# Half projections placed ahead of the turns of x, one transpose in another PSUM bank, and a tie on the sixth row of W_out

## The chip, the cores and the metric

The kernel is one program on one core of a Trainium2 chip. The core has a matrix engine (PE, whose weight loads are listed apart as PEld), a vector engine (DVE), a scalar engine (ACT), a general engine (POOL), and a queue (SP) that does nothing in this kernel but start transfers between the chip's large memory and the on-chip memory SBUF. PE writes its results to PSUM, which has eight banks. Each engine works through its own list of instructions in order and waits at an instruction until the data and the buffers that it needs are there.

The metric is the time of one launch in microseconds on the device. Lower is better. Three runs of the kernel before gave 1722.09, 1722.20 and 1724.09 us, so the median is 1722.2 us.

## The reference

One decoder layer over 1024 tokens with 16 learned tokens in front, width 1024:

```python
xn = rms_norm(h, mix_pre_g[l])
proj = xn @ w_in[l]                       # z, xbc, dt, q, k, v
y_ssd = ssd_mixer(z, xbc, dt_raw, ...)    # 16 heads, chunks of 128, state 128, causal conv of 4
y_sb = rms_norm(stick_breaking_attention(q, k, v), sb_norm_g[l])   # 16 heads of 64
mix = jnp.concatenate([y_ssd, y_sb], axis=-1) @ w_out[l]
h = h + rms_norm(mix, mix_post_g[l])
xn = rms_norm(h, ffn_pre_g[l])
gu = xn @ w_up[l]
g = causal_dwconv(gu[..., :D_FF], ffn_conv_w[l], ffn_conv_b[l])
f = (jax.nn.gelu(g, approximate=True) * gu[..., D_FF:]) @ w_down[l]
h = h + rms_norm(f, ffn_post_g[l])
```

Everything is float32. In stick-breaking attention the weight of key s for query t is sigmoid(q.k/8) times the product of (1 - sigmoid) over the keys between s and t; a scan along the keys gives the product.

## The kernel before

**Products.** Large products run in a fast 32-bit mode. Each operand is split into a high part (a rounded copy, made on ACT) and a low part (the rest, made on DVE or POOL), and three products high-high, low-high and high-low are summed in one PSUM bank. So every block of weights costs a load into `wraw` (two buffers), a copy on ACT (`wh`) and a subtraction (`wl`).

**The head (lines 310 to 348).** x is loaded in nine pieces: the 16 learned tokens and eight blocks of 128. For each piece i, ACT sums the squares, POOL makes the root, DVE scales the piece into `xn` (line 276, two buffers), PE turns it in eight transposes (`turn_x`, line 288, `xtp`), ACT copies the high part and DVE subtracts the low part (lines 293 and 295) into `xs`. `xs` has three thirds of 400, 384 and 256 tokens: pieces 0 to 3, 4 to 6, and 7 and 8. Between the turns PE also projects the first third for dt, for block B0 and for block C0. `conv_chain(..., True)` gives a projection in half chains of 12 matmuls each (line 169, `pj_B` and `pj_C`); the second half of a third ends with a copy on ACT (line 215). In this stretch the order of every engine is written out by hand: what the code traces first is issued first. In the kernel before, the half chains come at the end of iterations 5 to 8, behind `turn_x` of the same iteration.

**The scan (lines 482 to 712).** Convolved B, C and x blocks are turned to token order by `to_tokens`: three parts, one transpose of 16 tokens and twice four transposes of 128, each part in a bank of the pair `tp` and copied out by DVE (lines 487 and 492, `tt_B`). The pair `z` serves the decay matrices of the scan (`sg`, line 634). Outside the hand-written stretches a planner orders the instructions when the program is built, from costs that it assumes, and an instruction can be issued ahead of others that were traced before it.

**Attention and W_out (lines 770 to 1080).** Eight head pairs p, eight query blocks i, written (p,i). A block has its score matmuls (`z`, line 782, in the pair of double banks `zz`), two sigmoids on ACT (`kp` and `bt`, lines 783 and 784), a scan on DVE (line 790), products on POOL (lines 792 and 793), then two blocks later its weights are turned on PE (`tw`, line 804, also in `zz`) and copied by ACT (`th`, line 806), and one block after that multiplied with v (`av`, line 819). PE's order is written out by hand here; that of ACT, DVE and POOL is the planner's. While the last two head pairs run, the first half of W_out is prepared: eight rows of blocks, each a load into one of the two `wraw` buffers (line 892), a scaled copy on ACT (line 904) and a subtraction on DVE (line 905). `STAGE` sets after which block each row is traced: row 5 at (6,6), row 6 at (6,7), row 7 at (7,0), row 8 at (7,1). Rows 7 and 8 take the place of the last third of `xs`, which is free once v of the last pair is projected. The row that is traced at (6,6) stands inside `tc.issue_after(copied[0])`, which keeps its ACT instruction behind the latest `th` copy that was traced; at (6,6) that is the last copy of block (6,4), at (6,7) the last copy of block (6,5).

**After that** come the two halves of W_out, the up projection with seven products per pair of blocks in place of eight, and the down projection, all bound by PE.

Of the kernel before, what the change touches and what calls it, by code (L numbers as in the profile page):

```python
# [17 lines left out]
P = 128  # L18
# [39 lines left out]
def tile_layer(ctx: ExitStack, tc: tile.TileContext, x, meta, rows, parts,  # L58
# [22 lines left out]
    def psum_z(name):  # L81
        return stage[0][1].tile([P, 512], F32, tag="z", name=name, bufs=2)
# [7 lines left out]
    def psum_tp(name):  # L90
        return stage[0][1].tile([P, 4, P], F32, tag="tp", name=name, bufs=tp_bufs[0])
# [68 lines left out]
    def project_steps(w, ncol, chunks, evac, name, halves_=False, skip=0):  # L160
        hi, lo = w
        for c0, n in chunks:
            s = skip if c0 == 0 else 0
            acc = psum_mm(f"pj_{name}_{c0}")
            for k in range(KB):
                if halves_ and k == KB // 2:
                    yield
                for j, (a, b) in enumerate(((hi, 0), (hi, 1), (lo, 0))):
                    mm(acc[:ncol, :n - s], a[:, k, :ncol], xs[c0][:, b, k, s:n],  # L169
                       start=(k == 0 and j == 0), stop=(k == KB - 1 and j == 2))  # L170
            evac(acc, c0 + s, n - s)
            yield

    def run(steps, n=None):
        for _ in steps if n is None else zip(range(n), steps):
            pass
# [33 lines left out]
    def conv_chain(b, nm, w, halves_=False):  # L210
        raw = rp.tile([P, L + 3], F32, tag="rq", name=f"craw_{nm}", bufs=3)
        nc.gpsimd.memset(raw[:, 0:3], 0.0)

        def ev(acc, c0, n):
            nc.scalar.activation(raw[:, 3 + c0:3 + c0 + n], acc[:, :n], AF.Copy)

        return raw, project_steps(w, P, CH, ev, nm, halves_)
# [13 lines left out]
    with tc.tile_pool(name="pre", bufs=3, side="right") as pre, \  # L231
            tc.manual_schedule(engines={ET.PE, ET.Activation, ET.DVE, ET.Pool, ET.SP}):
        spans = [(0, NM)] + [(NM + i * P, P) for i in range(NT)]
        xts = []

        def load_x(i):
            xts.append(pre.tile([P, D], F32, tag="xt", name=f"xt{i}", bufs=9))
            nc.sync.dma_start(out=xts[i][:spans[i][1]], in_=meta if i == 0 else x[(i - 1) * P:i * P, :])

        def raw_of(name, src):  # L240
            raw = wp.tile([P, KB, P], F32, tag="wraw", name=f"wr_{name}")
            nc.sync.dma_start(out=raw, in_=src)
            return raw

        load_x(0)
        load_x(1)
        gpre = row_bcast(pre, 0, D, "gpre")
        load_x(2)
        load_x(3)
        load_x(4)  # L250
        raw_dt = wp.tile([P, KB, 16], F32, tag="wraw", name="wr_dt")
        nc.sync.dma_start(out=raw_dt, in_=w_dt)
        raws = {"B0": raw_of("B0", w_xbc[8])}
        for i in range(5, NT + 1):
            load_x(i)
        raws["C0"] = raw_of("C0", w_xbc[10])
        nc.sync.dma_start(out=pp, in_=parts)

        sums, roots, norms = {}, {}, {}

        def square(i):
            if i <= NT:
                nr = spans[i][1]
                junk = pre.tile([P, D], F32, tag="junk", name=f"junk{i}", bufs=2)
                sums[i] = pre.tile([P, 1], F32, tag="ss", name=f"ss{i}")
                nc.scalar.activation(junk[:nr], xts[i][:nr], AF.Square, scale=D ** -0.5, accum_out=sums[i][:nr])

        def root(i):
            if i <= NT:
                roots[i] = rstd_of(pre, sums[i][:spans[i][1]], 1, spans[i][1], f"pre{i}")  # L270

        def norm(i):
            if i <= NT:
                nr = spans[i][1]
                norms[i] = pre.tile([P, D], F32, tag="xn", name=f"xn{i}", bufs=2)
                nc.vector.scalar_tensor_tensor(norms[i][:nr], xts[i][:nr], roots[i][:nr], gpre[:nr],
                                               op0=ALU.mult, op1=ALU.mult)

        def turn_x(i):
            c0, nr = spans[i]  # L280
            tps = []
            for hf in range(2):
                tp = (psum_tp, psum_z, psum_sd)[(2 * i + hf) % 3](f"xtp{i}_{hf}")
                if (2 * i + hf) % 3:
                    tp = tp.rearrange("p (a b) -> p a b", b=P)
                for b in range(4):
                    k = 4 * hf + b
                    nc.tensor.transpose(tp[:, b, :nr], norms[i][:nr, k * P:(k + 1) * P], ident[:nr, :nr])
                base = max(a for a, _ in CH if a <= c0)
                h, l = (xs[base][:, j, 4 * hf:4 * hf + 4, c0 - base:c0 - base + nr] for j in range(2))  # L290
                tps.append((tp, h, l))
            for tp, h, _ in tps:
                nc.scalar.activation(h, tp[:, :, :nr], AF.Copy)
            for tp, h, l in tps:
                nc.vector.tensor_tensor(l, tp[:, :, :nr], h.bitcast(F32), op=ALU.subtract)

        ws = {}

        def split_hi(name):
            hi = wp.tile([P, KB, P], F32R, tag="whi", name=f"wh_{name}", bufs=WB)  # L300
            lo = wp.tile([P, KB, P], F32R, tag="wlo", name=f"wl_{name}", bufs=WB)
            nc.scalar.activation(hi, raws[name], AF.Copy)
            ws[name] = hi, lo

        def split_lo(name, part):
            ks = slice(4 * part, 4 * part + 4)
            nc.gpsimd.tensor_tensor(ws[name][1][:, ks], raws[name][:, ks], ws[name][0][:, ks].bitcast(F32),
                                    op=ALU.subtract)

        chains = []  # L310
        for i in range(3):
            square(i)
            root(i)
        norm(0)
        norm(1)
        for i in range(NT + 1):
            if i == 4:
                run(dt_chain, 1)
            if i not in (2, 3):
                norm(i + 2)  # L320
            turn_x(i)
            if i != 2:
                square(i + 2 if i == 3 else i + 3)
                root(i + 2 if i == 3 else i + 3)
            if i == 3:
                norm(4)
                norm(5)
            if i == 1:
                hl = wp.tile([P, KB, 32], F32R, tag="whi", name="wh_dt", bufs=WB)
                nc.scalar.activation(hl[:, :, 0:16], raw_dt, AF.Copy)  # L330
                nc.gpsimd.tensor_tensor(hl[:, :, 16:32], raw_dt, hl[:, :, 0:16].bitcast(F32), op=ALU.subtract)
                dt_chain = dt_steps(hl)
            if i in (3, 4):
                split_hi("B0" if i == 3 else "C0")
            if i in (3, 4, 5):
                split_lo("B0" if i < 4 else "C0", int(i == 5))
            if i == 3:
                square(6)
                root(6)
                split_lo("B0", 1)  # L340
            if i == 3:
                chains.append(conv_chain(8, "B0", ws["B0"], True))
            if i in (5, 6):
                run(chains[0][1], 1)
            if i == 6:
                chains.append(conv_chain(10, "C0", ws["C0"], True))
            if i in (7, 8):
                run(chains[1][1], 1)

    halves = (slice(0, 64), slice(64, 128))  # L350
    M0 = NM - 2
# [111 lines left out]
    with tc.tile_pool(name="ssd", bufs=1, side="right") as sp:  # L463
# [17 lines left out]

        def to_tokens(src, dst, nm):
            for part in range(3):
                tp = psum_tp(f"tt_{nm}_{part}")
                if part == 0:
                    nc.tensor.transpose(tp[:NM, 0, :], src[:, 0:NM], ident)
                    nc.vector.tensor_copy(dst[:NM, 0, :], tp[:NM, 0, :])
                else:
                    for b in range(4):
                        t = 4 * (part - 1) + b  # L490
                        nc.tensor.transpose(tp[:, b, :], src[:, NM + t * P:NM + (t + 1) * P], ident)
                    nc.vector.tensor_copy(dst[:, 1 + 4 * (part - 1):5 + 4 * (part - 1), :], tp)
# [517 lines left out]
    copied = [None]  # L1010
# [4 lines left out]
    for p in range(8):  # L1015
        for i in range(NT):
# [40 lines left out]
                edge = edge_turn(p - 1)  # L1057
            for _ in range(2):
                if wsteps and len(wres) < min(8, 3 * left[0], STAGE.get((p, i), 0)):
                    with tc.issue_after(copied[0]) if (p, i) == (6, 6) else ExitStack():  # L1060
                        run(wsteps, 1)
            if wsteps and first is None and len(wres) == 8:
                run(wsteps)
# [743 lines left out]
    for s in range(n2):  # L1807
        n, a, b, p = steps2[s]
# [29 lines left out]
        for _ in range(2 if s > 5 and s % 2 else 1):  # L1838
            if wload and (wload[0][0] is not None or s > 5):
                pool, nm, k = wload.pop(0)  # L1840
# [87 lines left out]
```

## Time and profile before

| | |
|---|---|
| median of three runs | 1722.2 us |
| the profiled execution | 1724.05 us |
| its span, first to last instruction | 1722.1 us |
| around the span | 1.95 us |
| mean granted PE clock | 0.999 |
| PE busy | 1699.6 us |
| DVE busy | 1105.8 us |
| POOL busy | 833.9 us |
| ACT busy | 821.0 us |

In the lines of the profile below, a row of the timeline has the start in us, the duration in us, the engine, the line of the kernel, the operation, what it writes and reads, the shape, and how many like it were merged; in square brackets stands how long the engine was idle just before and what ended that. "SPq" is the queue of transfers. The profile infers the releaser from the semaphore that came last, and says that where the engine named had long been done it was another.

### The profile page before, as it was taken

How to read it: one execution, taken by the hardware profiler on the slowest of the kernel's cores; microseconds unless marked ns; L12 is line 12 of the kernel's file. 1: busy time of each engine (PE TensorE's matmuls, PEld its weight loads, DVE VectorE, ACT ScalarE, POOL GpSimd, SP SyncE). 2: the span in 40 equal slices, each digit the busy share in tenths (PEclk: the TensorE clock that was granted, in tenths of full speed). 3: DMA queues.
4: the chain of work that ended last, by engine and by line, in shares of the span. 5: the costliest groups of instructions: out<-in, count | busy, mean ns of one | idle time of the engine just before them, and what ended most of it. 6: DMA issues, size and time to landing. Idle time of an engine off the chain costs nothing. (4 is left out here: it accounts for less than half of the span.)

```text
span 1722.1 us, 28048 instructions
## 1 busy us (share of the span) xinstructions
PE 1699.6 (99%) x11230; PEld 1495.4 (87%) x11230; DVE 1105.8 (64%) x1234; ACT 821.0 (48%) x1370; POOL 833.9 (48%) x641
## 2 busy tenths in 40 slices
PE   7999999999999999999999999999999999999998
PEld 6999889888989998998788788999988888887886
DVE  6752973875676677577530667675666666659777
ACT  5423663554566566557653344433333333344544
POOL 4323664585566575565552222587767777300001
PEclk9999999999999999999999999999999999999999
DMA  4232333231011111112214553233322223395345
GB/s 164 56 114 93 109 124 111 68 104 38 26 38 38 33 31 38 38 50 76 76 66 153 208 172 123 68 111 110 105 92 92 92 92 103 122 327 177 105 115 177
DMA packets 90674, 173.87 MB, mean 101 GB/s; under 512 B 10704, under 2 KB 35816, under 8 KB 90544
## 3 DMA queue, kind: packets, MB, share of 16 engines
q1 hardware_dynamic: 90544, 172.08, 31.3%
q8 instruction: 88, 1.44, 0.3%
q14 instruction: 42, 0.34, 0.1%
HBM read 122.32 MB, written 49.73 MB: 100 GB/s over the span
## 5 line engine op out<-in xcount | busy, mean ns | idle before, releaser
L792 POOL TENSOR_TENSOR bt<-bt,kp 128x256 f32<-128x256 f32 (+7 forms) x128 | 212.0, 1675 | 184.5 <-DVE kp L790 143.6
L790 DVE TENSOR_TENSOR_SCAN kp<-kp,hold 128x272 f32<-128x272 f32 (+7 forms) x128 | 183.4, 1473 | 24.6 <-ACT kp L783 14.3
L1287 POOL TENSOR_TENSOR wlo<-wr,whi 128x1024 fp32r<-128x1024 f32 x43 | 99.3, 2318 | 42.7 <-ACT whi L1286 42.7
L1785 POOL TENSOR_TENSOR fms<-fms 128x1 f32<-128x1 f32 x8 | 2.9, 362 | 223.7 <-ACT dh L1670 197.0
L783 ACT ACTIVATE kp<-z 128x288 f32<-128x288 f32 (+6 forms) x112 | 82.7, 739 | 50.8 <-PE z L782 25.8
L1286 ACT ACTIVATE whi<-wr 128x1024 fp32r<-128x1024 f32 x43 | 45.7, 1064 | 111.2 <-PE fX L1337 67.5
L169 PE MATMUL pj_v<-xs,wh_v 128*128 128x400 f32 (+2 forms) x384 | 95.0, 334 | 0.0
L169 PE MATMUL pj_k<-xs,wh_k 128*128 128x400 f32 (+2 forms) x384 | 94.6, 333 | 0.0
L169 PE MATMUL pj_q<-xs,wh_q 128*128 128x386 f32 (+2 forms) x384 | 93.9, 331 | 0.0
L806 ACT ACTIVATE th<-tw 128x1024 f32<-128x1024 f32 (+2 forms) x96 | 75.5, 815 | 37.5 <-PE tw L804 37.3
L1670 ACT ACTIVATE dh<-ar 128x512 fp32r<-128x512 f32 x77 | 48.5, 630 | 93.2 <-PE dnB L1748 44.7
L169 PE MATMUL pj_X<-xs,wh_X 128*128 128x400 f32 (+2 forms) x384 | 92.0, 327 | 0.0
L169 PE MATMUL pj_z<-xs,wh_z 128*128 128x386 f32 (+2 forms) x384 | 91.6, 326 | 0.0
L1409 DVE SCALAR_TENSOR_TENSOR ga<-gr,pp,ga 128x1024 f32<-128x1024 f32 x44 | 69.0, 1567 | 34.4 <-ACT ga L1402 33.6
L758 DVE CAST qh<-q 128x128 fp32r<-128x128 f32 x64 | 46.5, 727 | 69.1 <-PE z L782 68.7
L976 PE MATMUL mo<-woa,yh 128*128 128x512 f32 x256 | 85.5, 400 | 0.0
L1671 DVE TENSOR_TENSOR dl<-ar,dh 128x512 fp32r<-128x512 f32 x77 | 53.2, 691 | 50.2 <-ACT dh L1670 50.1
L784 ACT ACTIVATE bt<-z 128x288 f32<-128x288 f32 (+6 forms) x112 | 83.1, 742 | 0.0
L804 PE MATMUL tw<-ident,bt 128*128 128x128 f32 x576 | 75.7, 274 | 2.2 <-POOL cb L793 1.7
L819 PE MATMUL av<-th,v 128*64 128x128 f32 x1152 | 77.2, 278 | 0.0
L819 PEld LDWEIGHTS av<-th,v 128*64 128x64 f32 x1152 | 61.6, 137 | 13.8 <-issue 10.9
L804 PEld LDWEIGHTS tw<-ident,bt 128*128 128x128 f32 x576 | 65.4, 141 | 8.7 <-issue 3.1
(560 smaller groups left out, 5603.9 us busy)
## 6 DMA issues: line engine op xcount, KB each, us to landing
wr<-in_w_up SPq DMA_DIRECT2D x44, 512.0 KB
fds<-ga SPq DMA_DIRECT2D x44, 256.0 KB
b<-in_w_down SPq DMA_DIRECT2D x44, 256.0 KB
ar<-fds SPq DMA_DIRECT2D x44, 256.0 KB
fda<-ga SPq DMA_DIRECT2D x33, 256.0 KB
ar<-fda SPq DMA_DIRECT2D x33, 256.0 KB
yk<-yd SPq DMA_DIRECT2D x16, 512.0 KB
wor<-in_w_out SPq DMA_DIRECT2D x12, 512.0 KB
```

Of the source, the lines that this page charges most:

```text
L169: mm(acc[:ncol, :n - s], a[:, k, :ncol], xs[c0][:, b, k, s:n], start=(k == 0 and j == 0), stop=(k == KB - 1 and j == 2))
L783: nc.scalar.activation(kp[:, :, a:a + w], z[:, :, :w], AF.Sigmoid, scale=-QSCALE)
L784: nc.scalar.activation(bt[:, :, a:a + w], z[:, :, :w], AF.Sigmoid, scale=QSCALE)
L790: nc.vector.tensor_tensor_scan(kp[:, j][:, ::-1], kp[:, j][:, ::-1], hold[:, L - n:L][:, ::-1], 0.0, op0=ALU.mult, op1=ALU.max)
L792: nc.gpsimd.tensor_tensor(bt[:, j, 0:m], bt[:, j, 0:m], kp[:, j, 1:m + 1], op=ALU.mult)
L804: nc.tensor.transpose(tw[:, j, b, :], bt[:, j, c0:c0 + P], ident)
L806: copied[0] = nc.scalar.activation(th[:, :, :nb, :], tw[:, :, :nb, :], AF.Copy).ins
L819: mm(av[halves[j], :], v[:, kb, halves[j]], th[:, j, b, :], start=kb == 0, stop=kb == i)
L976: recent[0] = mm(acc, u[:, k, :], v[:, cs], start=(k == 0 and j == 0), stop=(k == 7 and j == 2))
L1287: nc.gpsimd.tensor_tensor(l, raw, h.bitcast(F32), op=ALU.subtract)
L1409: nc.vector.scalar_tensor_tensor(v, self.g[jj][:, :, i:i + 256], fconv_w[:, j, i:i + 1], v, op0=ALU.mult, op1=ALU.add)
L1671: sub(lo[:, k], raw, hi[:, k].bitcast(F32), op=ALU.subtract)
```

## The change

Three edits. In the head, the half chains move from the end of an iteration to the place ahead of its `turn_x`, and the object for C0 (with the clearing of three columns on POOL) is made in iteration 7. In `to_tokens`, the first part of B of the second group goes to a bank of the pair `z`. In the attention, the row of W_out that is traced at (6,7) is tied behind the latest `th` copy as well.

```diff
             if i not in (2, 3):
                 norm(i + 2)
+            if i in (5, 6):
+                run(chains[0][1], 1)
+            if i == 7:
+                chains.append(conv_chain(10, "C0", ws["C0"], True))
+            if i in (7, 8):
+                run(chains[1][1], 1)
             turn_x(i)
...
                 chains.append(conv_chain(8, "B0", ws["B0"], True))
-            if i in (5, 6):
-                run(chains[0][1], 1)
-            if i == 6:
-                chains.append(conv_chain(10, "C0", ws["C0"], True))
-            if i in (7, 8):
-                run(chains[1][1], 1)
...
             for part in range(3):
-                tp = psum_tp(f"tt_{nm}_{part}")
+                if part == 0 and nm == "B1":
+                    tp = psum_z(f"tt_{nm}_{part}").rearrange("p (a b) -> p a b", b=P)
+                else:
+                    tp = psum_tp(f"tt_{nm}_{part}")
...
-                    with tc.issue_after(copied[0]) if (p, i) == (6, 6) else ExitStack():
+                    with tc.issue_after(copied[0]) if (p, i) in ((6, 6), (6, 7)) else ExitStack():
                         run(wsteps, 1)
```

## The prediction

> **What bounds the kernel now.** I read the head of the page first, then the table of waits of PE, then the timelines of PE, ACT, DVE, POOL and the transfer queue around each wait.
>
> ```profile
> span 1722.1 us, 28048 instructions
> PE 1699.6 (99%) x11230; PEld 1495.4 (87%) x11230; DVE 1105.8 (64%) x1234; ACT 821.0 (48%) x1370; POOL 833.9 (48%) x641
> ```
>
> PE is busy in 1699.6 of 1722.1 us. An edit that removes no PE work can only win some of the 22.5 us in which PE stands still, and 8.5 of those lie before the first turn. The table of PE's waits (total, times, longest) has the others that the change aims at:
>
> ```profile
> PE xtp L288 <- DVE xn L276: 10.3, 5, 8.5
> PE tw L804 <- POOL cb L793: 1.7, 1, 1.7
> PE tw L804 <- ACT bt L784: 0.5, 1, 0.5
> ```
>
> In the first row 8.5 of the 10.3 us are that start; the largest of the rest is in the first part below, and the wait of the second part is 0.48 us.
>
> **Half chains ahead of the turns.** The timeline of PE in the head: piece 4 (counted from 0), piece 5, the first half chain of B0, piece 6, the second half chain, and dt of the second third at the end.
>
> ```profile
> 18.77 1.06 PE L288 MATMUL xtp<-ident,xn 128*128 128x128 f32 x8 [0.25 <-DVE xn L276]
> 20.99 1.06 PE L288 MATMUL xtp<-ident,xn 128*128 128x128 f32 x8 [1.15 <-DVE xn L276]
> 21.81 0.61 PE L169 MATMUL pj_B<-xs,wh_B 128*128 128x400 f32 x2
> 24.08 1.04 PE L288 MATMUL xtp<-ident,xn 128*128 128x128 f32 x8
> 24.87 0.61 PE L169 MATMUL pj_B<-xs,wh_B 128*128 128x400 f32 x2
> 33.28 2.95 PE L226 MATMUL pj_dt<-xs,wh_dt 128*32 128x384 f32 x16
> ```
>
> Nothing is removed or added; PE idles 1.15 us because xn of piece 5 comes late. From start to start, a turn takes 24.87 - 24.08 = 0.79 us and a half chain 24.08 - 21.81 = 2.27 us (0.19 per product), so piece 4 gives way at 19.56, and 1.43 us pass until 20.99. With the half chain first, PE needs the first third of `xs` and both halves of the B0 weights then. On DVE and POOL:
>
> ```profile
> 13.76 3.67 DVE L295 TENSOR_TENSOR xs<-xtp,xs 128x512 fp32r<-128x512 f32 x6
> 17.35 3.49 DVE L276 SCALAR_TENSOR_TENSOR xn<-xt,rs_pre,gpre 128x1024 f32<-128x1024 f32 x2
> 21.61 2.30 DVE L276 SCALAR_TENSOR_TENSOR xn<-xt,rs_pre,gpre 128x1024 f32<-128x1024 f32 x1 [0.29 <-POOL rs_pre L196]
> 25.03 1.94 DVE L276 SCALAR_TENSOR_TENSOR xn<-xt,rs_pre,gpre 128x1024 f32<-128x1024 f32 x1
> 17.74 2.02 POOL L307 TENSOR_TENSOR wl_B<-wr_B,wh_B 128x512 fp32r<-128x512 f32 x1
> 21.54 1.29 POOL L307 TENSOR_TENSOR wl_B<-wr_B,wh_B 128x512 fp32r<-128x512 f32 x1
> 24.61 1.29 POOL L307 TENSOR_TENSOR wl_C<-wr_C,wh_C 128x512 fp32r<-128x512 f32 x1
> ```
>
> The first third is whole at 17.43 and the low half of B0's first part at 19.76; the third product of the chain is the first to use it, at 19.56 + 0.38 = 19.94. So the chain runs from 19.56 to 21.83, piece 5 (xn ready at 20.84) to 22.62, the second half chain to 24.89 (its first use of the low part is at 23.00, ready at 22.83), piece 6 (xn ready at 23.91) to 25.68, the first half chain of C0 (low part ready at 25.90, used at 26.06) to 27.95, piece 7 (xn ready at 26.97). Nothing is late again, and dt of the second third starts at 33.28 - 1.43 = 31.85. The tightest margins are 0.16 to 0.18 us, so a slip costs tenths. What moves on the other engines: ACT's copy of B0 and that of C0 stand ahead of the copies of pieces 6 and 8, but PE makes their inputs in that same order. POOL's clearing for C0 keeps its place, and no transfer is passed. xn of piece 7 takes the buffer of piece 5, which PE now leaves at about 22.9 in place of 22.1, well ahead of DVE's 25.03. Gain: 1.15 us by the idle column, 1.43 by the starts; below it zero, if work later in line has a clock of its own.
>
> **First part of B of the second group in a bank of z.** PE, and DVE beside it:
>
> ```profile
> 310.02 0.42 PE L169 MATMUL pj_q<-xs,wh_q 128*128 128x386 f32 x1
> 310.92 0.66 PE L491 MATMUL tt_B<-ident,bt 128*128 128x128 f32 x4 [0.48 <-DVE bn L487]
> 308.57 2.11 DVE L478 SCALAR_TENSOR_TENSOR ct<-craw_C,pp,ct 128x784 f32<-128x784 f32 x2
> 310.59 0.27 DVE L487 COPY bn<-tt_B 16x128 f32<-16x128 f32 x1
> ```
>
> The third part needs the first part's bank, whose copy is queued on DVE behind the convolution of C until 310.59. With the first part in z, the second and third have the two tp banks to themselves and PE goes on. The z banks are idle between the scans, and the copy frees the bank at 310.86. Gain: 0.48 us by the idle column; by the starts 310.92 - 310.02 less one product of 0.19, 0.71. No price on the other side that the rows show.
>
> **Sixth row of W_out behind a copy.** The rows that explain the two waits at `tw`:
>
> ```profile
> 799.85 0.33 SPq L892 DMA_DIRECT2D wor<-in_w_out  x1
> 804.62 1.15 ACT L904 ACTIVATE woa<-wor,pp 128x1024 fp32r<-128x1024 f32 x1 [1.99 <-DMA wor<-in_w_out]
> 807.69 0.93 ACT L784 ACTIVATE bt<-z 128x912 f32<-128x912 f32 x1
> 809.32 0.95 ACT L784 ACTIVATE bt<-z 128x912 f32<-128x912 f32 x1
> 806.75 0.28 PE L169 MATMUL pj_k<-xs,wl_k 128*128 128x256 f32 x1
> 808.72 1.06 PE L804 MATMUL tw<-ident,bt 128*128 128x128 f32 x8 [1.69 <-POOL cb L793]
> 810.32 0.44 PE L804 MATMUL tw<-ident,bt 128*128 128x128 f32 x2 [0.53 <-ACT bt L784]
> 811.45 1.21 ACT L904 ACTIVATE woa<-wor,pp 128x1024 fp32r<-128x1024 f32 x1
> ```
>
> The weights that are turned at 808.72 are those of block (6,4), whose POOL products ended long before, so the table's "POOL cb" is not the cause. A turn takes a `zz` bank, and both hold the scores of (6,6) until ACT has read them: the first `bt` ends at 808.62, the second at 810.27, just ahead of the two turns. ACT is late because it stood 1.99 us before 804.62 for a W_out row that was still landing, then spent 1.15 us on it. That is the sixth row: the fifth is tied behind the copies of (6,4), so it can only be the one at 811.45. Tied, the sixth gives ACT these 3.1 us back, `kp` of (6,6) can start with its scores at about 804, and its `bt` end before PE's 806.87 and 807.66. Gain: 1.69 + 0.53 = 2.22 us by the idle column; by the starts 808.72 - 806.75 - 0.12 and 810.32 - 808.72 - 0.79, together 2.66.
>
> What is late next: the row's ACT copy moves from 804.62 to behind the last `th` of (6,5), its subtraction on DVE likewise, and the load of row 8, which takes its `wraw` buffer, behind that.
>
> ```profile
> 820.68 0.59 ACT L806 ACTIVATE th<-tw 128x512 f32<-128x512 f32 x1
> 819.49 4.54 DVE L790 TENSOR_TENSOR_SCAN kp<-kp,hold 128x1040 f32<-128x1040 f32 x2
> L905 DVE SCALAR_TENSOR_TENSOR woa<-wor,pp,woa x8: 1279/1556/3092, 777.4 to 829.3; 128x1024 fp32r<-128x1024 f32 x8
> 823.54 1.73 ACT L806 ACTIVATE th<-tw 128x1024 f32<-128x1024 f32 x2
> 825.19 1.75 PE L819 MATMUL av<-th,v 128*64 128x128 f32 x28
> 828.99 0.62 ACT L783 ACTIVATE kp<-z 128x544 f32<-128x544 f32 x1 [3.23 <-POOL cb L793]
> 831.55 1.09 PE L804 MATMUL tw<-ident,bt 128*128 128x128 f32 x8
> 838.07 0.48 PE L976 MATMUL mo<-woa,yh 128*128 128x512 f32 x1
> ```
>
> All of these come 2.66 us earlier with PE. The sixth copy is then done by 820.68 + 0.59 - 2.66 + 1.15 = 819.8. DVE is in the scan of (6,7) until 819.49 + 4.54 - 2.66 = 821.4; the subtraction behind it takes 1.28 to 3.09 us and ends at 822.7 to 824.5. The load then takes as long as the sixth row's own, 804.62 - 799.85 = 4.77, so row 8 lands at 827.4 to 829.2, is copied by 830.4 and subtracted by 833.4. PE first multiplies with it at 838.07 - 2.66 = 835.4, so 2 us are left and the move costs nothing, unless row 8's copy stands in ACT's list ahead of something that PE needs sooner. That is the open price, 0 to 10 us, taken up under the rivals; I take 0, because PE's own deadline is the nearest bound and the planner has cause to issue row 8 late.
>
> The subtraction of row 6 took longer than 1.28 us when POOL worked beside it, up to 3.09. The Trainium skill (SBUF — State Buffer, Who interferes with whom) says that a DVE instruction with two SBUF inputs and a POOL instruction that reads SBUF exclude each other for the whole instruction. That speaks against the move into a stretch full of POOL products: by that rule one could wait out a product of the (6,7) block, and the end of row 8 would come about a microsecond later than by the rows, still ahead of PE.
>
> **The sum.** Idle column: 1.15 + 0.48 + 2.22 = 3.85. Starts: 1.43 + 0.71 + 2.66 = 4.80. I take 4.4, nearer to the starts, which are recorded, while ends are modelled. The Trainium skill (Perfetto Trace Analysis, Identifying the Most-Contended Engine) calls matmul busy time a bad measure since pipelined instructions look smaller; by it the idle column counts for nothing and the sum would be 4.80.
>
> The profiled execution took 1724.05 us, the span and 1.95 around it, so it would take 1719.65. It lies 1.85 above the median, with the run of 1724.09. Two stretches of 4 us show where such a difference can come from (PE busy in the third column, granted clock before the share of DMA):
>
> ```profile
> 1068.00:1072.00 4.00, 2.02 (x13) 1.29 (x11) 3.43 (x4) 1.99 (x4) 0.44 (x1) 0.98 0.31 73
> 1072.00:1076.00 4.00, 3.89 (x21) 3.89 (x22) 2.27 (x4) 1.66 (x4) 0.00 (x0) 0.60 0.14 58
> ```
>
> After a pause of 2 us PE runs 4 us at a clock of 0.60, which costs 1.6 us. The change does not touch that place; an estimate from these rows is that some executions escape the drop. From the median of 1722.2 the forecast is 1722.2 - 4.4 = 1717.8.
>
> **The rivals.**
> 1. All gaps close, but the runs after fall on the upper of the two levels: 1717.8 + 1.9 = 1719.7. One of three runs and the profiled one were there.
> 2. The wait moves from row 6 to row 8. If its copy is listed ahead of `kp` of (7,1), the two sigmoids end at 829.8 to 831.6 (row 8 landing, 1.15 for its copy, twice 0.62) in place of 828.99 - 2.66 + 1.24 = 827.6, and the turn of (6,7), which needs that `zz` bank at 831.55 - 2.66 = 828.9, waits 0.9 to 2.7 us. Left is 4.4 less that, 1718.7 to 1720.5. The sixth row itself shows that the planner lists such copies too early.
> 3. Slower: the same copy is listed ahead of the `th` copies of (6,6), which stood at 823.54, 2.9 us behind the `th` that row 6 is tied to. ACT then holds them until row 8 has landed and is copied, 828.6 to 830.4, and they end 1.73 later at 830.3 to 832.1; `av` needs them at 825.19 - 2.66 = 822.5. PE stands 7.8 to 9.6 us where 4.4 were won: 1725.6 to 1727.4. It decides as soon as the planner assumes less than 2.9 us between the two for a subtraction and a load. Against it: the load alone takes 4.77 us.
> 4. The edits shift the planner's clock and it lists the scan stage or the attention differently: PE is 99% busy there, so a new order can lose more than win, 1719 to 1726.
>
> **How the numbers follow.** Forecast 0.45; rival 1 0.13, rival 2 0.20, rival 3 0.14, rival 4 0.08. A measurement of this kernel can tell about 0.2% (3.4 us) from no change. Faster by more, below 1718.8: the forecast and a little of rival 2, 0.48. Within it: rival 1, most of 2 and a part of 4, 0.30. Slower, above 1725.6: rival 3, the rest of 2 and 4, 0.22. The likeliest case's own range is 1717.2 to 1718.6; the range given, 1716.8 to 1726.5, holds rivals 1 and 2 and most of 3.
>
> **What would show it.** Right: the waits of 1.15, 0.48, 1.69 and 0.53 are gone from PE's table; dt of the second third starts near 31.85; at (6,6) ACT goes from `th` to `kp` with no wait on W_out; PE busy stays near 1699.6 while the span falls by 4 to 5 us. Wrong: a wait on `wor` on ACT between 820 and 832 with PE idle at `av` or `tw` behind it, a new PE gap before 50 us, or more idle PE in the scan stage.

## The result, and the profile after

| | before | after |
|---|---|---|
| median, measured side by side | 1724.09 us (11 runs) | 1728.03 us (11 runs) |
| range | 1721.37 to 1726.35 | 1725.57 to 1728.88 |
| the profiled execution | 1724.05 us | 1728.03 us |
| its span | 1722.1 us | 1726.0 us |

The ratio after to before is 1.002, 95% interval 1.0012 to 1.0027: the change makes the kernel slower, by about 3.4 us by the ratio and 3.9 by the medians. The forecast was 1717.8 us, 4.4 below the median that it started from. Three executions far longer than all others (4142.08 and 2106.84 us of the kernel before, 1852.78 us of e17) are left out of the ratios and of the medians below.

The head of the page after. PE's busy time rose by 3.3 us though it has the same 11230 products, so part of the loss is not idle time.

```profile
span 1726.0 us, 28047 instructions
PE 1702.9 (99%) x11230; PEld 1498.0 (87%) x11230; DVE 1108.6 (64%) x1234; ACT 821.7 (48%) x1370; POOL 835.2 (48%) x641
```

PE's table of waits after (total, times, longest). The two waits at `tw` and that at `tt_B` are gone; those at `sg`, `av`, `z` and `pj_B` are new.

```profile
PE xtp L288 <- DVE xn L276: 8.9, 3, 8.6
PE sg L637 <- ACT sgh L628: 1.9, 2, 1.4
PE av L822 <- ACT th L809: 1.7, 1, 1.7
PE z L785 <- ACT th L809: 1.2, 1, 1.2
PE pj_B L169 <- POOL wl_B L307: 0.2, 1, 0.2
```

PE's list is the same in both kernels behind the head, but for one product of q that changes places with a transpose at 310 us. So the start of each of its products after, less its start before, is an offset, and a step of the offset shows where time was won or lost. In this pair of profiles: -1.00 us in the head, -0.69 at `tt_B`, **+5.40 at the start of the second group's scan** (318 to 330 us), -2.62 at (6,6), **+2.88 between 819 and 842 us**, +0.13 at 1072 to 1080; with +0.11 at the start that is +4.21.

**The scan.** The timeline after, and below it the same instructions before:

```profile
313.37 3.19 DVE L478 SCALAR_TENSOR_TENSOR ct<-craw_C,pp,ct 128x256 f32<-128x256 f32 x3
314.38 1.90 POOL L630 TENSOR_TENSOR sgl<-tri,adl 128x1024 fp32r<-128x1024 f32 x1 [1.19 <-PE sg L637]
314.00 0.20 PE L637 MATMUL sg<-sgh,lowr 16*16 16x64 f32 x1
316.59 0.42 ACT L480 ACTIVATE ct<-ct 128x256 f32<-128x256 f32 x1 [4.78 <-DVE ct L478]
318.93 2.43 ACT L628 ACTIVATE sgh<-tri,adh 128x128 fp32r<-128x128 f32 x8
320.24 0.50 PE L637 MATMUL sg<-sgh,lowr 128*128 128x512 f32 x1 [1.44 <-ACT sgh L628]
```

```profile
314.26 1.52 DVE L478 SCALAR_TENSOR_TENSOR ct<-craw_C,pp,ct 128x256 f32<-128x256 f32 x3
315.96 1.90 POOL L627 TENSOR_TENSOR sgl<-tri,adl 128x1024 fp32r<-128x1024 f32 x1 [1.89 <-PE sg L634]
315.59 0.20 PE L634 MATMUL sg<-sgh,lowr 16*16 16x64 f32 x1
318.15 2.44 ACT L625 ACTIVATE sgh<-tri,adh 128x128 fp32r<-128x128 f32 x8
```

POOL's `sgl` of chunk (1,1) waits until PE has read that of chunk (1,0). Before, it started at 315.96, just 0.18 us behind the last convolution of C on DVE (314.26 + 1.52 = 315.78). After, PE skips the wait at `tt_B`, reads `sg` earlier against DVE, and POOL starts at 314.38, into the convolution. By the view of that line, one of the three DVE instructions took 2145 ns in place of 485 (minimum, median, maximum):

```profile
L478 DVE SCALAR_TENSOR_TENSOR ct<-craw_C,pp,ct x3: 485/485/2145, 313.4 to 314.4; 128x256 f32<-128x256 f32 x3
```

ACT's list then runs in order: the activation of C, a copy of q, a table load of 1.28 us, `em`, `sgh`. All come late and PE stands 1.44 and 0.44 us at `sg`. Behind it the clock is halved (windows; the granted clock is the third number from the right):

```profile
321.00:325.00 4.00, 3.58 (x9) 1.88 (x10) 2.48 (x2) 4.00 (x13) 1.90 (x1) 0.66 0.02 4
325.00:329.00 4.00, 4.00 (x21) 4.00 (x21) 1.47 (x3) 0.11 (x1) 1.42 (x1) 0.50 0.00 0
```

**The attention.** The transfer queue, ACT, DVE and PE after; then the queue before:

```profile
818.88 0.33 SPq L895 DMA_DIRECT2D wor<-in_w_out  x1
831.39 0.33 SPq L895 DMA_DIRECT2D wor<-in_w_out  x1
833.09 0.33 SPq L955 DMA_DIRECT2D yk<-yd  x1
822.47 1.15 ACT L907 ACTIVATE woa<-wor,pp 128x1024 fp32r<-128x1024 f32 x1 [1.51 <-DMA wor<-in_w_out]
834.91 1.15 ACT L907 ACTIVATE woa<-wor,pp 128x1024 fp32r<-128x1024 f32 x1 [2.28 <-DMA wor<-in_w_out]
837.42 1.06 ACT L964 ACTIVATE yh<-yk 128x1024 fp32r<-128x1024 f32 x1 [1.20 <-DMA yk<-yd]
823.53 0.58 ACT L809 ACTIVATE th<-tw 128x512 f32<-128x512 f32 x1
838.39 1.92 ACT L809 ACTIVATE th<-tw 128x1024 f32<-128x1024 f32 x2
828.27 3.09 DVE L908 SCALAR_TENSOR_TENSOR woa<-wor,pp,woa 128x1024 fp32r<-128x1024 f32 x1
824.16 0.66 PE L822 MATMUL av<-th,v 128*64 128x128 f32 x8 [1.67 <-ACT th L809]
839.45 0.45 PE L785 MATMUL z<-kh,qh 64*128 64x400 f32 x2 [1.24 <-ACT th L809]
```

```profile
808.17 0.33 SPq L892 DMA_DIRECT2D wor<-in_w_out  x1
816.38 0.33 SPq L892 DMA_DIRECT2D wor<-in_w_out  x1
```

A row holds its `wraw` buffer until its subtraction is done, and which row follows in which buffer is settled when the program is built. Before, row 7 takes the buffer that row 6's early copy and subtraction free, at 808.17, and row 8 that of row 5, at 816.38. With row 6 tied, row 7 takes row 5's buffer and waits for its subtraction, until 818.88. Row 8 takes the same buffer behind row 7, whose subtraction ends at 828.27 + 3.09 = 831.36, so its load starts at 831.39. Row 6's buffer goes to the third block of y, at 833.09. ACT's list has row 7's copy (822.47) ahead of the second `th` of (6,5) (823.53), and now row 8's copy (834.91) ahead of the `th` copies of (6,7) (838.39), with `yh` of the third block of y between them. So ACT holds `th` while rows land, and PE stands 1.67 and 1.24 us: what was won at (6,6) goes.

### The profile page after: what moved, and what is told of

Its sections match the earlier page's. It is cut to its first block, busy times and chain, and to the rows that moved or that the text cites. A ratio compares the mean times of both kernels' runs of the same rounds, so it can differ in the third digit from the quotient of the medians.

```text
span 1726.0 us, 28047 instructions
## 1 busy us (share of the span) xinstructions
PE 1702.9 (99%) x11230; PEld 1498.0 (87%) x11230; DVE 1108.6 (64%) x1234; ACT 821.7 (48%) x1370; POOL 835.2 (48%) x641
## 3 DMA queue, kind: packets, MB, share of 16 engines
q8 instruction: 88, 1.44, 0.3%
## 5 line engine op out<-in xcount | busy, mean ns | idle before, releaser
L169 PEld LDWEIGHTS pj_q<-xs,wh_q 128*128 128x128 f32 x384 | 66.4, 194 | 5.5 <-issue 5.4
```

## Experiments

Each was timed side by side with the kernel before; line numbers shift by a few between kernels. A ratio of 0.001 is 1.7 us.

| run | what | ratio, 95% interval |
|---|---|---|
| e1_head | head alone | 0.9988 (0.9980 to 0.9997) |
| e2_bank | bank alone | 1.0012 (1.0004 to 1.0021) |
| e3_tie | tie of row 6 alone | 1.0006 (0.9996 to 1.0016) |
| e4_bank_sgl | bank, `sgl` on DVE | 0.9994 (0.9985 to 1.0003) |
| e6_tie67 | ties of rows 6, 7 | 0.9987 (0.9977 to 0.9996) |
| e7_tie678 | ties of rows 6 to 8 | 0.9999 (0.9991 to 1.0008) |
| e8_after_sgl | whole change, `sgl` on DVE | 0.9995 (0.9986 to 1.0004) |
| e9_bank_fill | bank, filler products | 1.0011 (1.0002 to 1.0020) |
| e12_tie9 | rows 6 to 8 and `yh` tied | 0.9991 (0.9982 to 1.0000) |
| e13_head_tie9 | the same and the head | 0.9977 (0.9967 to 0.9987) |
| e14_head_tie67 | head, rows 6 and 7 | 0.9986 (0.9977 to 0.9995) |
| e15_all9 | e13, the bank, `sgl` on DVE | 0.9972 (0.9960 to 0.9983) |
| e16_after_fill | whole change, filler | 1.0009 (0.9999 to 1.0018) |
| e17_after_again | whole change again | 1.0016 (1.0008 to 1.0025) |

### Each edit alone

e1 moves the half chains and nothing else (the first two hunks of the change, cut here):

```diff
+            if i in (5, 6):
+                run(chains[0][1], 1)
...
             turn_x(i)
```

> The kernel before with the half chains ahead of the turns alone. Theory A (the head gives what it should, and the loss at the start of the second scan belongs to the bank): PE's wait of 1.15 us ahead of piece 5 is gone, PE is about 1.0 us ahead from dt of the second third on and stays so, no wait at sg, the clock stays at 1.0 at 320 to 330 us; time 1 us below before. Rival B (being early is what upsets the second scan): the waits at sg (1.9 us) and the drop of the clock show here too, time 3 to 4 us above before.

The offset is about -1.1 us from 100 us on up to the attention, and no wait at `sg` appears. The edit does what it was expected to.

e2 moves the bank and nothing else (the diff is cut here):

```diff
+                if part == 0 and nm == "B1":
+                    tp = psum_z(f"tt_{nm}_{part}").rearrange("p (a b) -> p a b", b=P)
```

> The kernel before with the first part of B's turn in a bank of z alone. Theory A: PE's wait of 0.48 us at tt_B is gone, PE reaches the first sg about 0.7 us early, POOL starts the next sgl while DVE is still in the last part of the convolution of C, DVE's three instructions there take 3.2 us in place of 1.5, PE waits 1.9 us at sg and runs some 7 us at half the clock; time about 4.7 us above before. Rival B: no wait at sg, time 0.7 us below before. Rival C (the drop of the clock is chance): the waits at sg are there, the clock stays, time about 1.2 us above before.

The offset falls 0.69 at `tt_B` and rises 3.86 behind it. PE waits 1.9 us at `sg`, in two waits as in the whole change, and the clock falls behind them:

```profile
325.00:327.00 2.00, 2.00 (x10) 1.89 (x10) 2.00 (x2) 1.87 (x7) 0.95 (x1) 0.53 0.00 0
```

So the loss in the scan comes with this edit alone; the head isn't needed for it.

e3 ties row 6 and nothing else:

```diff
-                    with tc.issue_after(copied[0]) if (p, i) == (6, 6) else ExitStack():
+                    with tc.issue_after(copied[0]) if (p, i) in ((6, 6), (6, 7)) else ExitStack():
```

> The kernel before with the tie of the sixth row alone. Theory A (the wait moves to rows 7 and 8): PE gains 2.6 us at tw of (6,4), loses 1.6 at av of (6,5) behind ACT's wait for row 7's load and 1.3 at the scores of (7,2) behind its wait for row 8's; time within 0.5 us of before. Rival (the other two edits make rows 7 and 8 late): the gain of 2.6 us stays, time 2.6 us below before.

Won at (6,6): 2.62. Given back at these two places: 3.04 of offset.

```profile
822.86 0.66 PE L819 MATMUL av<-th,v 128*64 128x128 f32 x8 [1.81 <-ACT th L806]
838.15 0.45 PE L782 MATMUL z<-kh,qh 64*128 64x400 f32 x2 [1.24 <-ACT th L806]
```

These runs also showed that the gain at (6,6) was too large in the one profile of before. In e1, e2, e4 and e9 row 6 is not tied, and yet the offset falls 1.0 to 1.2 us at (6,6). In e1:

```profile
798.76 7.14 SPq L892 DMA_DIRECT2D wor<-in_w_out  x2
802.35 1.15 ACT L904 ACTIVATE woa<-wor,pp 128x1024 fp32r<-128x1024 f32 x1 [0.81 <-DMA wor<-in_w_out]
806.46 1.07 PE L804 MATMUL tw<-ident,bt 128*128 128x128 f32 x8 [0.51 <-issue]
```

The load took 802.35 - 798.76 = 3.59 us there (3.6 to 3.7 in the other three), not the 4.77 of before's profile. So by four of the five profiles in which row 6 is not tied, the tie wins about 2.6 - 1.1 = 1.5 us; how often an execution is like the fifth is not known.

### The collision in the scan

e4 is e2 with `sgl` of chunk (1,1) on DVE; e8 is the whole change with the same edit:

```diff
-            nc.gpsimd.tensor_tensor(sgl[:nr, :, :nr], tri...
+            (nc.vector if (g, c) == (1, 1) else nc.gpsimd).tensor_tensor(sgl[:nr, :, :nr], tri...
```

> The kernel with the bank alone, and the low part of the decay arguments (sgl) of the first full chunk of the second group on DVE in place of POOL. Theory A (POOL beside DVE's two-input instructions makes the loss): DVE's three instructions at the end of the convolution of C take 1.5 us again, no wait at sg over 0.3 us, the clock stays at 1.0, time 0.7 us below before, less what the extra 1 to 2 us of DVE work may cost. Rival (the late table load and sgh on ACT make it, whatever POOL does): the waits at sg and the drop of the clock stay, time 4 to 5 us above before.

> The whole change, with the low part sgl of chunk (1,1) made on DVE and not on POOL. Theory A (the loss in the scan is POOL's sgl beside the DVE convolution of C, the pause of PE and the slow clock behind it): DVE's convolution instructions back at 1.5 us each, the waits of 1.44 and 0.44 at sg shrink to 0.5 or less, clock above 0.95 from 321 to 329, and the time lies 4 to 5 us under that of the whole change (1728), at 1723 to 1724; against before -1.0 from the head, 0 from the bank (its 0.7 is given back at sg), +0.3 from the tie: ratio 0.9996. Rival B (PE comes to the scan 1.6 us earlier and would wait for ACT's sgh whatever POOL does): a wait of 1.4 or more at sg stays, slow clock behind it, 1726 to 1728.

In e8 the convolution is back at its length, ACT's `sgh` starts at 317.27 in place of 318.93, and only the small wait is left:

```profile
313.37 1.53 DVE L478 SCALAR_TENSOR_TENSOR ct<-craw_C,pp,ct 128x256 f32<-128x256 f32 x3
315.93 1.20 DVE L630 TENSOR_TENSOR sgl<-tri,adl 128x1024 fp32r<-128x1024 f32 x1
317.27 2.44 ACT L628 ACTIVATE sgh<-tri,adh 128x128 fp32r<-128x128 f32 x8
319.76 0.50 PE L637 MATMUL sg<-sgh,lowr 128*128 128x512 f32 x1 [0.42 <-ACT sgh L628]
```

The clock stays at 1.00 from 317 to 333, and the offset rises by 0.69 at `sg` in place of 5.40 (0.70 in e4). Two things follow. The collision of POOL with DVE is the cause of the loss; and without it the 0.7 us of the bank are still taken back at `sg`, because ACT makes `sgh` no sooner: it starts at 318.18 in e4 and at 318.15 in the kernel before, and at 317.27 in e8, which has the head's gain. The bank never had a gain to keep.

### Is the half clock part of it?

e9 is e2, e16 the whole change, with filler products in the pause:

```diff
                 pz = psum_z(f"sg{nm}_{j}").rearrange("p (a b) -> p a b", b=P)
+                for _ in range((6, 2)[j] if (g, c) == (1, 1) else 0):
+                    mm(pz[:, 0:3, :].rearrange("p a b -> p (a b)"), lowr, xs[0][:, 0, 0, 0:384], start=True, stop=True)
```

> The bank of z alone, and in the pause of PE ahead of the sg products of chunk (1,1) six products of 384 columns into the same bank, two more ahead of the second half; the real products overwrite them. Nothing is left out of the result. Theory A (3.5 of the 5 us lost there come from the slow clock, and that from the pause of PE): the pause is filled, clock above 0.95 from 321 to 329, the q products at 0.28 and 0.40 us, the offset against the kernel before rises at sg by about 2 us and not by 4 to 5, ratio 1.0002 or below. Rival B (the clock falls there for another reason, the load of DVE, ACT and POOL or the place in the program): clock 0.5 to 0.7 for some us as with the bank alone, ratio 1.0012.

> The whole change with six and two filler products ahead of the sg products of chunk (1,1), as in the run of the bank with filler. Theory A (the pause of PE brings the half clock, in every execution): clock above 0.95 from 321 to 329, the loss at the start of the scan falls from 5.4 to 2.0 us, ratio 1.0000 and 3 us below the whole change run in the same call. Rival B (the clock falls there only in a part of the executions, by chance, as it does at 874 and 1072 in some): the two profiles may differ, but the times of the two kernels agree within their intervals.

> The whole change once more, beside the run with filler, on the same chip. Theory A: a pause of 1.4 and 0.4 us at sg, the clock at 0.5 to 0.7 from about 322 to 329 as in the first profile, ratio 1.002. Rival B: the pause is there and the clock stays at 1.00 in this execution.

In e16 the filler closes the pause to 0.16 us and the clock stays up:

```profile
318.73 1.33 PE L637 MATMUL sg<-xs,lowr 128*128 128x384 f32 x6 [0.16 <-ACT em L641]
320.00 0.50 PE L639 MATMUL sg<-sgh,lowr 128*128 128x512 f32 x1
```

```profile
325.00:329.00 4.00, 4.00 (x39) 3.38 (x38) 2.42 (x6) 2.48 (x6) 3.16 (x3) 1.00 0.00 0
```

In e17, without it:

```profile
325.00:329.00 4.00, 4.00 (x24) 4.00 (x24) 2.72 (x3) 1.37 (x5) 1.87 (x2) 0.66 0.00 0
```

The loss in the scan is 2.35 (e9) and 2.37 (e16) with filler, 3.86 (e2), 3.88 (e17) and 5.40 (the first profile of after) without. So of the loss 0.7 is the bank's own gain given back, 2.36 - 0.7 = 1.7 the delay of one DVE instruction (2145 - 485 ns = 1.66), and 1.5 to 3.0 the clock, which is halved for 3.41 us in e2 and e17 and for 6.83 us in the first profile of after. In the times this is weaker: e16's median is 1.7 us under e17's, 1725.75 against 1727.47, as theory A would have it, but the intervals of the ratios overlap, and e9's ratio of 1.0011 is that of e2, against the expectation. The mean clock of the single runs is on record too: it is 0.997 or less in 20 of the 22 runs of the whole change (after and e17) and in 3 of the 12 of e16. The counts of e2 and e9, 4 of 11 and 2 of 10, separate nothing. That all three profiles with the pause show the half clock and neither with filler does is shown; that every execution has it is not.

### Where the wait for W_out goes

e6 ties row 7 too, e7 rows 7 and 8 (the line shortened):

```diff
-  ... if (p, i) in ((6, 6), (6, 7)) else ExitStack():
+  ... if (p, i) in ((6, 6), (6, 7), (7, 0)) else ExitStack():            # e6
+  ... if (p, i) in ((6, 6), (6, 7), (7, 0), (7, 1)) else ExitStack():    # e7
```

> The tie alone, on rows 5, 6 and 7 (row 7 is the one traced at (7,0)). Theory A (each W_out row that ACT takes before it has landed makes PE wait; a tie removes the wait of its own row and leaves that of the next untied one): the wait at av for th, 1.6 to 1.8 us in the runs with row 6 alone tied, is gone, the wait at z for th near 839 (1.2 to 1.3 us, row 8) stays; the offset against the kernel before falls by 2.6 at (6,6) and gives 1.3 back, -1.3 us net, ratio 0.9992. Rival B (the load, copy and subtraction of a row take so long that a tie only moves one and the same wait to the next place): the av wait goes but its 1.7 us come back at tw, z or mo of (6,7) to (7,2), net +0.3, ratio 1.0002.

> The tie alone, on rows 5 to 8. Theory A: neither the wait at av for th nor that at z for th, all of the 2.6 us stay won at the first product of W_out, ratio 0.9985. Rival B: PE waits 1 to 3 us for woa at the first products of W_out or for th of (6,7) behind row 8, ratio 0.9995 or above.

e6: the wait at `av` for row 7 is gone, and 0.48 at `z` with 1.03 at the next `av` stand behind row 8 and `yh`; 1.81 of offset given back (A said 1.3; B's net of +0.3 would be 2.9). e7: here A fell. Row 8 holds nothing up, but PE loses 1.67 behind the next untied copy, of y:

```profile
836.41 1.06 ACT L961 ACTIVATE yh<-yk 128x1024 fp32r<-128x1024 f32 x1 [4.04 <-DMA yk<-yd]
838.43 1.09 PE L819 MATMUL av<-th,v 128*64 128x128 f32 x16 [1.44 <-ACT th L806]
```

That load takes the `wraw` buffer of row 7. The wait walks along the two buffers, from row 6 to 7, to 8, to y. e12 ties this copy too:

```diff
                 if i == 1 and t < NT - 1:
-                    ys.append(split_y(wp, 0, t + 2, ("whi", "wlo", WB)))
+                    with tc.issue_after(copied[0]) if t == 1 else ExitStack():
+                        ys.append(split_y(wp, 0, t + 2, ("whi", "wlo", WB)))
```

> The tie alone, on rows 5 to 8 of W_out, and the copy yh of the third block of y (its load takes the wraw buffer of row 7) tied behind the last th copy of (6,7) as well. Theory A (the wait walks along the wraw buffers: row 6, row 7, row 8, then this block; ACT is held wherever the next untied copy stands ahead of a th): no wait above 0.5 us at av, z or tw between 800 and 860, the 2.6 us won at (6,6) stay, ratio 0.9986. Rival B (the chain of loads, copies and subtractions itself is too late for PE by then, wherever the copies stand): PE waits 1 us or more behind kp of (7,2), at tw or at the products of W_out, net -1 us, ratio 0.9995.

ACT in e12 now has the last `th` of (6,7), row 8 and `yh` in this order; `yh` still waits 1.63 us, and nobody waits for it:

```profile
830.72 1.03 ACT L806 ACTIVATE th<-tw 128x1024 f32<-128x1024 f32 x1 [0.21 <-PE tw L804]
831.78 1.15 ACT L904 ACTIVATE woa<-wor,pp 128x1024 fp32r<-128x1024 f32 x1
834.57 1.06 ACT L961 ACTIVATE yh<-yk 128x1024 fp32r<-128x1024 f32 x1 [1.63 <-DMA yk<-yd]
```

PE has no wait between 800 and 860 us and keeps all of the 2.62. The ratio of 0.9991 is 1.5 us, the size found above. The times alone don't rank the ties: e6, whose profile gives 1.81 back, has 0.9987, and the intervals overlap. Chance in the clock is larger than that difference: the mean clock is 0.997 or less in 5 of e12's 11 runs and in none of e6's 10.

### Versions that beat both

> The same with the head's edit, without the bank. Theory A: -1.0 from the head and -2.6 from the ties, ratio 0.998, median 3.5 us under the kernel before. Rival B: one microsecond from each, ratio 0.9988.

> The head's edit with rows 5, 6 and 7 tied, without the bank and with nothing of y moved. From the single runs: -1.0 from the head, -1.0 from the ties (2.6 won at (6,6), 1.5 given back behind row 8): ratio 0.9988; waits of 0.5 at z for th and 1.0 at av for th. If the two edits disturb one another (the planner lists the attention otherwise), another wait stands there and the ratio is 0.9995 or above.

> All three edits with what they ran into taken away: sgl of chunk (1,1) on DVE, rows 5 to 8 of W_out and the copy yh of the third block of y tied. Theory A (the bank wins nothing that sg does not take back): no wait above 0.5 between 800 and 860, one of 0.4 at sg, the same as head and ties without the bank, ratio 0.9978. Rival B (the 0.7 us of the bank can be kept): ratio 0.9974, offset 0.6 lower from 330 on than with head and ties alone.

e13 (head of e1 and ties of e12) has an offset of -3.69 at 860 us, no new wait, and a median of 1720.47 against 1724.77. e14 keeps the waits of e6 (0.59 at `z`, 0.98 at `av`) and loses 1.84 there: the two edits don't disturb one another. e15 adds the bank with `sgl` on DVE; its offset at 330 us is -0.96, that of e13 -1.07, so the bank adds nothing, and 0.9972 is not told apart from 0.9977. The version to take is e13, which has fewer edits than e15.

## Why the prediction was wrong

- **Head: right in its mechanism.** Forecast 1.15 to 1.43, won 1.00. dt of the second third starts at 32.38, not 31.85: half chains wait up to 0.15 for POOL's `wl_B`, the margin called tight.

```profile
20.46 0.45 PE L169 MATMUL pj_B<-xs,wl_B 128*128 128x400 f32 x1 [0.15 <-POOL wl_B L307]
32.38 1.80 PE L226 MATMUL pj_dt<-xs,wh_dt 128*32 128x384 f32 x9
```

- **Bank: the step that failed is "No price on the other side that the rows show."** The gain at `tt_B` was right, 0.69 against 0.48 to 0.71, but e4 and e8 show that `sg` takes all of it back. Only the engine that waited was followed. What PE releases when it comes sooner is POOL's `sgl`, which stood 0.18 us behind the convolution, and what PE needs next is ACT's `sgh`. The price was put at nothing and measured 5.40 in the profile (3.86 and 3.88 in e2 and e17). The rule that the prediction weighed for the tie bore on this place: the Trainium skill (SBUF — State Buffer, Who interferes with whom) makes such a DVE instruction and POOL exclude each other for the whole instruction. The trace agrees: beside POOL's instruction of 1.90 us, the DVE instruction of 485 ns took 1.66 us longer.
- **Tie: the step that failed is "the move costs nothing", with "I take 0, because PE's own deadline is the nearest bound."** The 2.62 won at (6,6) met the forecast of 2.22 to 2.66, though only about 1.5 of it is there in four of five profiles. The buffers were traced wrongly: row 8 does not take row 6's. Before, row 7 does, as the queue's start at 808.17 showed, right behind row 6's subtraction (805.80 + 2.34 = 808.14). With row 6 tied, rows 7 and 8 both follow in row 5's buffer, so row 7 is late too, and its copy stands ahead of a `th`. Row 8's load was put at 822.7 to 824.5 and started at 831.39; PE was 3.9 us later there than the prediction assumed, so 3 to 5 us of that are the chain of buffers. Price 2.88 against 0. One reading was off as well: the subtraction of 3.09 us is row 7's, row 6's took 2.34. Rivals 2 and 3 had the mechanism, ACT held by an untied copy, but for row 8 alone; it came at two places, smaller than rival 3 and larger than rival 2.
- **Rival 4 did not happen**: in the scan DVE, ACT and POOL keep their order, and in the attention only rows 6 and 8 of W_out and two copies beside them change places.
- **The level.** The forecast subtracted from 1722.2, the median of three runs. The kernel before has medians of 1724.1 to 1725.1 in the later, larger sets, so 2 of the 10.2 us of error are the starting point. That some executions escape the drop of the clock near 1072 us was right: 10 of the 16 profiles do. Of the rest, the head's and the ties' own gains were near their forecasts; the prices of 5.40 and 2.88 turned -4.4 into +3.9.

## What to carry to other kernels

When an edit lets an engine go sooner, list what that engine releases and check each released instruction against what runs on the other engines then: here 0.18 us, by luck, separated a POOL instruction from a DVE convolution. A wait for a load is a property of the chain of buffers, not of the row that happens to show it: moving one copy moved the wait to the next copy in the chain, and it took four ties before none stood ahead of what PE needed. A single profile's wait for a transfer may be a microsecond off from most executions; so read it in a second run before building a sum on it.

## What the hardware showed beside that

The half clock also comes in places that no edit touches, and not in every execution. Between 1068 and 1080 us, behind the same two pauses of about 1 us each, it cost 1.4 us in 6 of the 16 profiles (before, after, e1, e6, e8, e14) and nothing in the others. Near 874 to 884 us it cost 1.5 us in 6 (e1, e3, e12, e14, e16, e17), with no wait of PE in the table for that place. In the head of e3 and e7, which ran 2.4 us longer, it made 1.5 of that, and in e8 it came at 819.7 us behind a wait of 2.33 us at `av`. Much of the 3 to 5 us over which the runs of one kernel spread goes with it: of the kernel before, 42 runs with a mean clock of 0.999 took 1723.02 us on average, 51 with 0.998 took 1724.95 and 19 with 0.997 took 1726.68.

The traces show where it comes. In each of the 16 the clock changes only on a raster of 3.41 us: in the kernel before it is whole for 1058.13 us, which is 310 times 3.41, halved for 3.41 and whole again for 645.12, which is 189 times. Where the raster lies against the program differs from execution to execution. Take as idle share of one such stretch the time in which PE stands still or runs products of at most 16 rows. It is 0.50 to 0.62 in all 19 stretches with the half clock behind them; in the others up to 1705 us, some 7900, it reaches 0.50 at most, with one exception of 0.53 (e4, near 871 us). Before, both pauses near 1070 us fall into one stretch, in which PE is busy 1.61 of 3.40 us, and the clock behind it is 0.50; in e2 they fall into two, the emptier one has 1.98 of 3.40, and the clock stays:

```profile
1068.40:1071.80 3.40, 1.61 (x11) 0.98 (x9) 3.23 (x4) 1.39 (x3) 0.04 (x1) 1.00 0.30 60
1071.80:1075.20 3.40, 3.09 (x14) 3.09 (x15) 2.47 (x4) 1.86 (x4) 0.00 (x0) 0.50 0.23 94
```

```profile
1072.70:1076.10 3.40, 1.98 (x15) 1.78 (x16) 2.57 (x4) 2.09 (x4) 0.00 (x0) 1.00 0.51 154
1076.10:1079.50 3.40, 3.40 (x25) 3.17 (x24) 2.01 (x4) 1.78 (x5) 0.00 (x0) 1.00 0.00 0
```

Near 874 us the profile has PE busy without a break, but 1.94 us go into products of 16 rows and 4 columns; in e12:

```profile
871.38 1.94 PE L877 MATMUL avm<-wcm,meta_v 16*128 16x4 f32 x16
874.90:878.30 3.40, 3.40 (x20) 2.73 (x17) 1.36 (x1) 2.93 (x5) 0.63 (x4) 0.50 0.51 157
```

So the chance is, by this working, where the raster falls. It rests on ends that are modelled, and on a count of small products as idle that no run tested by itself. The Trainium skill (TensorE: Matmul & The Clock Gate, Part 1: The HAM clock gate) has the clock halved after an idle window of about 3.4 us that runs freely. The raster of 3.41 us and its changing place agree with that; but no stretch ahead of these 19 was idle throughout, and about half was enough.
